# Second half's values as Strassen pairs behind ten split gate pairs, in a decoder block on one core

## The chip, the cores and the metric

The kernel runs on one core of a Trainium2 chip. The metric is the device time of one execution in microseconds; the figure for a kernel is the median of its runs. A profile is one further execution recorded by the hardware profiler; its span reaches from the first to the last instruction.

## The reference

One decoder block over 2048 positions and 1024 channels, in float32. `h` is the normalised and modulated input; one projection with eight column groups of 1024 feeds everything that follows:

```python
mod = c_act @ w_mod[l] + b_mod[l]
h = rms_norm(x, g_norm[l]) * (1.0 + scale) + shift
proj = h @ w_in[l]
x_rnn, z_rnn, q, k, v, z_attn, g_r, g_a = jnp.split(proj, IN_SPLITS, axis=-1)
...  # convolution and gated recurrence over x_rnn, times silu(z_rnn), projected
...  # rotary embedding of 32 of 128 channels of q and k, attention of 8 heads, times silu(z_attn), projected
merged = sigmoid(g_r + bg_r) * y_rnn + sigmoid(g_a + bg_a) * y_attn
x = rms_norm(x + gate * (merged @ w_o[l]), g_final)
```

## The kernel before

**Number format.** Every float32 operand is held as a high and a low part, and a product is three matmuls on TensorE (`mm3`, L156): high times high, high times low, low times high. The high part is a rounding copy on ScalarE (`hi_act`, L162); the low part is a subtraction, on GpSimd (`lo_pool`, L168) or on VectorE (`lo_dve`, L171).

**Halves and banks.** The positions are worked on in two halves (`for f in range(2)`, L1463), each of two banks of 512 positions, the even and the odd one. B11 and B21 hold the upper and lower 512 channels of the even bank of h, B12 and B22 those of the odd bank. Each is a high and a low tile of 128 x (4 x 512), from a pool of 14 such slots (`T`).

**Strassen pairs.** A projection's columns are taken 256 at a time, as a pair of 128-column blocks. With the two halves of the 1024 input channels and the two banks this is a 2 x 2 block product, made from seven block products instead of eight (`strassen`, L375). In order they use B11, T2, T3, T1, B21, T4 and B22; T1 to T4 are sums of the four B operands. The left operands (numbers 0 to 6 of the pair) are the blocks a11, a12, a21, a22 of w_in and their sums. A block product is 4 x 3 matmuls of 128 x 128 by 512 columns. Product 0 leaves a sum in PSUM bank X; ScalarE copies it to `u1` (L410), and product 4 goes on adding in X, four products later. u2 and u3 are Z + u1 and W + u2, on VectorE. Product 6 is held back until the next pair's product 0 is through (`behind`, `last_product`). `done(i, j, ps, u)` ends output block i for bank j.

**Order of the work.** Every engine's instructions stand in the order of the program (a manual schedule). `n_prod` counts block products; after each, `run_late` (L222) issues what was put down for that count in `late`, `after_prod` and `events`. `later(d, fn)` and `steps_after` put work down d products ahead.

**Left operands.** In the first half a pair's blocks are loaded from w_in, summed on VectorE and split into `S` tiles, a ring of seven (`s_tile`, L195), four products ahead (`LEAD`). Raw blocks go through a ring of five (`raw_tile`). The split operands are stored to `sD`, but for operands 0, 4 and 5, which are plain blocks of w_in and are loaded and split anew in the second half (`is_raw`, L270), and but for the two pairs of `ANEW`, whose operands are all made again. In the second half `load_next` (L326) loads operand n as soon as operand n - 7 is used, on the queue of SyncE (SP), and `split_next` splits raw ones four products ahead.

**The pairs.** 28 pairs a half: eight recurrent ones, twelve gate ones (silu gate and the two merge gates), six plain ones and two rotated ones of q and k; the same order in both halves. A recurrent pair sets off some 19 products of steps, among them two small products with `w_a` and `w_x` into the two `pg` banks of PSUM (L1033) and their sigmoids one product later (L1038).

**Values.** The 1024 value columns aren't pairs. `value_runs` (L904) makes them with positions as rows: a run is 256 columns for one bank, 96 matmuls with 256 moving columns. In the second half `second_values` (L927) does eight runs before the first pair: four on the even bank, then four on the odd one. Meanwhile `build_odd` (L567) turns the odd bank's x (`turned`, four transposes on TensorE), makes B12, B22 and T1 to T4 and splits them. Its low parts are on VectorE but for B12's and B22's share and T3, which is on GpSimd (L586). The even bank is built during the last pair of the first half (`next_even`, L1434). Under the value runs go also `residual_gate` (L1326), 16 pieces of w_mod summed on VectorE, and the loads of the value columns. `rotary_tables` (L1086) and `output_weights` (L451), which splits both output projections into `wD`, run under the second half's pairs.

Of the kernel before, what the change touches and what calls it, by code (L numbers as in the profile page):

```python
# [20 lines left out]
P = 128  # L21
# [5 lines left out]
H = 8  # L27
# [62 lines left out]
def decoder_block(ctx, tc, x, c, positions, g_norm, w_mod, b_mod, w_in, b_gate, conv_w, conv_b,  # L90
# [176 lines left out]
    ANEW = (22, 27)  # L267
    loaders, unsplit = {}, []

    def is_raw(x, i):  # L270
        return i in PLAIN and x in loaders and not (i == 5 and x + 1 in ANEW)


    def operand_events(x, pieces, f=0):
# [9 lines left out]
        def split(i, name):  # L284
            if f:
                assert n_loaded[0] == 7 * x + i
                n_loaded[0] += 1
# [38 lines left out]
    def load_next():  # L326
        n = n_loaded[0]
        n_loaded[0] += 1
        if n < 28 * 7:
            t = s_tile([P, 2, KH, P])  # L330
            if is_raw(n // 7, n % 7):
                unsplit.append((n, t, loaders[n // 7](*PLAIN[n % 7])))
            else:
                nc.sync.dma_start(t[:].bitcast(F32), sD[n])
            loaded.append((n, t))
        else:
            k = n - 28 * 7
            if k < 3:
                load_wd(0, 0, k) if k < 2 else load_wd(0, 1, 0)
# [9 lines left out]
    def load_free():  # L349
        n = n_loaded  # L350
        while n[0] - NS in used and not (n[0] < 28 * 7 and n[0] // 7 in ANEW):
# [23 lines left out]
    def strassen(up, f, key, done):  # L375

        x = pair_id[key]
        if f and x == 0:
            while n_loaded[0] < NS:
                load_next()  # L380
            split_next(4)
        n_op = iter(range(7 * x, 7 * x + 7))

        def take():
            if f and x not in ANEW:
                return (f, *loaded.pop(0))
            i = next(n_op)
            return f, i, first.pop(i)

        def prod(ps, b, first, last, op=None):  # L390
            f, i, s = op or take()
            bh, bl = B[b]
            for k in range(KH):
                mm3(ps[:], s[:, 0, k, :], s[:, 1, k, :], bh[:, k, :], bl[:, k, :],
                    first=first and k == 0, last=last and k == KH - 1, skip_group_check=True)
            n_prod[0] += 1
            if f:
                used.add(i)
                load_free()
                split_next(i + 4)  # L400
            run_late(n_prod[0])
            if f:
                load_free()
                split_next(i + 4)

        X = T(pj, [P, CH], F32, "X", bufs=2)
        prod(X, "B11", True, False)
        last_product()
        u1 = T(up, [P, CH], F32, "u1", bufs=1)
        nc.scalar.activation(u1[:], X[:], AF.Copy)  # L410
        Z = T(pj, [P, CH], F32, "Z")
        prod(Z, "T2", True, True)
        u2 = T(up, [P, CH], F32, "u2", bufs=2)
        with tc.high_priority():
            nc.vector.tensor_tensor(u2[:], Z[:], u1[:], ALU.add)
        W = T(pj, [P, CH], F32, "W")
        prod(W, "T3", True, True)
# [3 lines left out]
        V = T(pj, [P, CH], F32, "V")  # L421
        prod(V, "T1", True, False)
        done(1, 1, V, u3)
        prod(X, "B21", False, True)
        done(0, 0, X, None)
        Y = T(pj, [P, CH], F32, "Y")
        prod(Y, "T4", True, True)
        done(1, 0, Y, u3)
        op = take()

        def last():
            prod(V, "B22", False, True, op)
# [4 lines left out]
    behind = []  # L437

# [12 lines left out]
    def output_weights():  # L451

        parts = [(i, w, m, half) for i, w in enumerate((w_out_rnn, w_out_attn)) for m in range(KT) for half in range(2)]
        for x, (i, w, m, half) in enumerate(parts):
# [17 lines left out]
            for d, fn in ((1, load), (4, split), (6, store)):  # L472
                after_prod.setdefault(n_prod[0] + 9 * x // 2 + d, []).append(fn)
# [92 lines left out]

    def build_odd(st, xs):  # L567

        B["B12"] = (T(st, [P, KH, CH], F32R, "b12h"), T(st, [P, KH, CH], F32R, "b12l"))
        operand("B22")  # L570
        f32 = lambda b, i, k: B[b][i][:, k, :].bitcast(F32)
        tt = nc.vector.tensor_tensor
# [7 lines left out]

        low = []

        def split(name, k, t):
            hh, hl = (b[:, k, :] for b in B[name])
            hi_act(hh, t)
# [1803 lines left out]
```

## Time and profile before

| what | value |
|---|---|
| runs | 2186.95, 2187.05, 2190.51 us; median 2187.05 |
| profiled execution | span 2189.4 us; no separate time of it beside the span is given |
| TensorE busy | 2156.2 us (98%), 11333 matmuls |
| VectorE, ScalarE, GpSimd busy | 1494.8, 1266.5, 1237.3 us |
| DMA | 513.91 MB, mean 235 GB/s |
| second half's values | 697.7 to 795.6 us |
| second half's pairs | 795.6 to 1353 us |

In a row of the profile PE is TensorE's matmul, PEld its weight load, DVE VectorE, ACT ScalarE, POOL GpSimd and SP SyncE, whose queue issues most DMAs. L154 is a line of the kernel; a helper's line (L154, L162, L168, L171) stands for all its callers, so the tiles' names say which work it is. A group's row ends with busy time, mean duration in ns and the idle time before it. In the order of time, the first number is the start and the second the duration, both in us; matmuls are pipelined, so the pace of a group is the distance between starts.

### The profile page before, as it was taken

The numbers are of one execution on the slowest core, as the hardware profiler recorded it, in microseconds if no ns is written. First come the engines' busy times: TensorE is split into PE (matmuls) and PEld (weight loads), VectorE is DVE, ScalarE is ACT, GpSimd is POOL, SyncE is SP. The second block draws the span as 40 slices with busy tenths as digits, with TensorE's granted clock in tenths as the row PEclk, the third lists the DMA queues.
The fourth block names the chain that finished last, engine by engine and source line by source line (L and its number), as shares of the span: only waits on it lengthen the run. The fifth ranks groups of instructions, "written<-read, shape, count | busy, mean of one in ns | idle before, by whom it ended". The sixth has DMA issues, their size and how long they took to land.

```text
span 2189.4 us, 34270 instructions
## 1 busy us (share of the span) xinstructions
PE 2156.2 (98%) x11333; PEld 1834.3 (84%) x11333; DVE 1494.8 (68%) x2456; ACT 1266.5 (58%) x2544; POOL 1237.3 (57%) x909
## 2 busy tenths in 40 slices
PE   8999999999999999999999999999999999999998
PEld 6998888888888998888888888888989898978787
DVE  6779888978576765455536556567677778746877
ACT  4547667667543447557567412677778887632443
POOL 2467767677567355445444324456565656433886
PEclk9999999999999999999999999999999999999999
DMA  8355665665997567887887899989988788799554
GB/s 297 103 171 195 216 198 190 205 216 192 266 269 226 164 190 252 249 252 236 261 258 243 264 295 294 286 268 276 279 274 270 239 261 256 223 295 274 182 170 135
DMA packets 454474, 513.91 MB, mean 235 GB/s; under 512 B 91192, under 2 KB 333588, under 8 KB 453528
## 3 DMA queue, kind: packets, MB, share of 16 engines
q1 hardware_dynamic: 422644, 429.45, 65.4%
q10 hardware_dynamic: 31460, 82.22, 9.9%
q8 instruction: 90, 1.47, 0.3%
q14 instruction: 88, 0.72, 0.1%
q0 software_dynamic: 192, 0.05, 0.0%
HBM read 337.52 MB, written 174.07 MB: 234 GB/s over the span
## 4 chain that ended last, share of the span: by engine, by line
PE 62%; DMA 8%; DVE 5%; issue 2%; ACT 2%; POOL 1%; SPq 1%; DVEq 0%; ACTq 0%; POOLq 0%
PE X L154 12%; PE V L154 11%; PE pj L154 9%; PE W L154 6%; PE Z L154 6%; PE Y L154 6%; PE sc L154 4%; PE o L154 4%; PE pg L154 1%; DMA vraw<-vN 1%; PE pT L1708 1%; PE pT L1721 1%; DMA mrT<-fg 1%; DMA or<-in_w_o_dram 1%; DMA or<-oD 1%
## 5 line engine op out<-in xcount | busy, mean ns | idle before, releaser
L168 POOL TENSOR_TENSOR S<-R,S 128x512 fp32r<-128x512 f32 x278 | 413.0, 1491 | 378.2 <-ACT S L162 320.2
L154 PE MATMUL V<-T,S 128*128 128x512 f32 x1344 | 324.4, 390 | 0.6 <-DVE xr L481 0.6
L154 PE MATMUL X<-T,S 128*128 128x512 f32 x1344 | 323.3, 389 | 0.2 <-POOL S L168 0.2
L154 PEld LDWEIGHTS X<-T,S 128*128 128x128 f32 x1344 | 252.0, 188 | 52.8 <-POOL S L168 0.7
L154 PEld LDWEIGHTS V<-T,S 128*128 128x128 f32 x1344 | 251.4, 188 | 52.9 <-DVE xr L481 1.0
L154 PE MATMUL pj<-yh,S 128*128 128x512 f32 x848 | 284.1, 394 | 1.4 <-ACT yh L162 0.8
L162 ACT ACTIVATE S<-R 128x512 fp32r<-128x512 f32 x278 | 171.6, 624 | 134.9 <-DMA R<-in_w_in_dram 88.2
L168 POOL TENSOR_TENSOR S<-s,S 128x512 fp32r<-128x512 f32 x114 | 183.1, 1606 | 99.2 <-ACT S L162 70.1
L154 PEld LDWEIGHTS pj<-yh,S 128*128 128x128 f32 x848 | 159.2, 188 | 34.0 <-ACT yh L162 1.6
L1624 ACT ACTIVATE pp<-pp,st 128x256 f32<-128x256 f32 (+3 forms) x256 | 133.9, 526 | 74.1 <-DVE st L1623 73.7
L154 PE MATMUL pj<-yl,S 128*128 128x512 f32 x424 | 165.3, 392 | 1.3 <-POOL yl L168 0.9
L154 PE MATMUL Y<-T,S 128*128 128x512 f32 x672 | 161.5, 389 | 0.0
L154 PE MATMUL W<-T,S 128*128 128x512 f32 x672 | 161.5, 389 | 0.0
L154 PE MATMUL Z<-T,S 128*128 128x512 f32 x672 | 161.4, 389 | 0.0
L154 PEld LDWEIGHTS Z<-T,S 128*128 128x128 f32 x672 | 126.1, 188 | 26.2
L154 PEld LDWEIGHTS Y<-T,S 128*128 128x128 f32 x672 | 126.1, 188 | 26.1
L154 PEld LDWEIGHTS W<-T,S 128*128 128x128 f32 x672 | 126.1, 188 | 26.1
L162 ACT ACTIVATE S<-s 128x512 fp32r<-128x512 f32 x114 | 71.4, 626 | 125.7 <-DVE s L299 63.5
L171 DVE TENSOR_TENSOR ptl<-pT,pth 128x384 fp32r<-128x384 f32 (+1 forms) x160 | 97.8, 628 | 50.8 <-ACT pth L162 48.6
L1025 DVE SCALAR_TENSOR_TENSOR xc<-xr,par,xc 128x512 f32<-128x512 f32 x96 | 98.1, 1022 | 50.2 <-ACT xc L1019 47.9
L1623 DVE CUSTOM_DVE_ANT_0 pp<-sc,msk 128x256 f32<-128x256 f32 (+3 forms) x256 | 104.2, 449 | 33.0 <-PE sc L154 30.7
L1688 ACT ACTIVATE pp<-pp,M 128x256 f32<-128x256 f32 (+3 forms) x256 | 118.6, 528 | 9.2 <-DVE M L1812 9.2
(400 smaller groups left out, 4818.3 us busy)
## 6 DMA issues: line engine op xcount, KB each, us to landing
sD<-S ACTq DMA_DIRECT2D x112, 512.0 KB, 3.6
S<-sD SPq DMA_DIRECT2D x112, 512.0 KB, 5.0
S<-wD SPq DMA_DIRECT2D x100, 512.0 KB, 6.2
R<-in_w_in_dram SPq DMA_DIRECT2D x195, 256.0 KB, 4.3
wD<-s ACTq DMA_DIRECT2D x64, 256.0 KB, 4.4
T<-in_w_mod_dram SPq DMA_DIRECT2D x8, 1024.0 KB, 9.6
vN<-ev SPq DMA_DIRECT2D x64, 128.0 KB, 2.7
zaT<-ev SPq DMA_DIRECT2D x32, 256.0 KB, 3.6
```

Source lines behind the costliest of these rows:

```text
L154: nc.tensor.matmul(o, lhsT=l, rhs=r, start=st, stop=sp, **kw)
L162: nc.scalar.activation(o, i, AF.Copy)
L168: nc.gpsimd.tensor_tensor(o, i, h.bitcast(F32), ALU.subtract)
L171: nc.vector.tensor_tensor(o, i, h.bitcast(F32), ALU.subtract)
L1025: nc.vector.scalar_tensor_tensor(xc, xr[:, i : i + CH], cw(i), xc, ALU.mult, ALU.add)
L1623: nc.vector.tensor_tensor_reduce(pdst, s_ps, mask, 1.0, 3e38, ALU.add, ALU.min, m_)
L1624: nc.scalar.activation(pdst, pdst, AF.Exp, bias=m_, scale=-1.0, accum_out=l_)
L1688: nc.scalar.activation(pp, pp, AF.Copy, scale=w)
L1708: nc.tensor.transpose(pt[:, c0 + j * P : c0 + (j + 1) * P], pp[i][:, k * P : (k + 1) * P], ident)
L1721: nc.tensor.transpose(pt[:, c * P : (c + 1) * P], pp[:, half * P : (half + 1) * P], ident)
```

## The change

In the second half the values become four pairs (`("v", m)`) of seven products each. An output block of such a pair has channels as rows; it is evicted, turned by four transposes into a `pg` bank two products later, copied by ScalarE and stored (`value_done`). Their left operands are made anew from w_in (`ANEW`).

The second half starts with `second_heads`: ten of the twelve gate pairs do only their products 0 and 4, those with B11 and B21, two pairs at a time (X, X or Z, W). The first sums are kept in ten `u1h` tiles. These 20 products take the place of the value runs as the time in which the odd bank is built. `build_odd_late` makes no B12, takes 16 steps (after head products 6 to 21) and a rest after product 22, splits what a step made one and two products later, and gives the low parts of T1, T2 and T3 to GpSimd. Then the ten pairs' remaining five products follow (`strassen` with `u1`), with a changed use of PSUM banks (`body_tags`). `residual_gate`, `output_weights` (every 4 products instead of 4.5) and `rotary_tables` run under these. The remaining order of the second half is new: each recurrent pair is followed by one other, the last by two.

The loads of x for the odd bank and of the first seven operands move into the last pair of the first half. `ops2` lists the second half's operands in their order of use; `sD` is indexed by pair and operand.

```diff
-    ANEW = (22, 27)
+    N1 = 28 * 7
+    ANEW = (22, 27, 28, 29, 30, 31)
...
+    def heads(up, f, pairs):
+        U = []
+        Xs = [T(pj, [P, CH], F32, tag, bufs=1 + (tag == "X")) for tag in next(head_tags)]
+        for X, (key, _) in zip(Xs, pairs):
+            prod(take(f, pair_id[key], 0), X, "B11", True, False)
+            U.append(T(up, [P, CH], F32, "u1h", bufs=N_HEADS))
+            nc.scalar.activation(U[-1][:], X[:], AF.Copy)
+        for X, (key, done) in zip(Xs, pairs):
+            prod(take(f, pair_id[key], 4), X, "B21", False, True)
+            done(0, 0, X, None)
+        return U
+
+    def strassen(up, f, key, done, u1=None):
+        x, X = pair_id[key], None
+        if u1 is None:
+            X = T(pj, [P, CH], F32, "X", bufs=2)
+            prod(take(f, x, 0), X, "B11", True, False)
+            last_product()
+            u1 = T(up, [P, CH], F32, "u1", bufs=1)
+            nc.scalar.activation(u1[:], X[:], AF.Copy)
...
+        last_product()
...
+        tag = "V" if X is not None else next(body_tags)
+        V = T(pj, [P, CH], F32, tag, bufs=1 + (tag == "X"))
...
+    N_HEADS = 10
+    ODD_AT = tuple(range(6, 22))
+    body_tags = itertools.cycle(("V", "X", "X"))
+    head_tags = itertools.cycle((("X", "X"), ("Z", "W")))
...
-                after_prod.setdefault(n_prod[0] + 9 * x // 2 + d, []).append(fn)
+                after_prod.setdefault(n_prod[0] + 4 * x + d, []).append(fn)
...
+    def build_odd_late(st, up, xs):
...
+        def step():
+            ready = then[:]
+            then.clear()
+            for fn in soon:
+                then.append(fn())
+            soon.clear()
+            for fn in ready:
+                fn and fn()
+
+        def halves(name, k, t, low=True):
+            def hi():
+                hi_act(B[name][0][:, k, :], t)
+                return (lambda: lo_pool(B[name][1][:, k, :], t, B[name][0][:, k, :])) if low else None
+            soon.append(hi)
+
+        for k in range(KH):
+            build(st, ("B12", "B22"), xs, KH + k, keep=h[k])
+            pt = turned(xs, k)
+            nc.scalar.activation(h1s[:, k, :], pt[:].rearrange("p r j -> p (r j)"), AF.Identity,
+                                 bias=sh[:, k : k + 1], scale=gs[:, k : k + 1])
+            yield
...
+        for part, k in ("a0", "b0", "a1", "b1", "a2", "b2", "a3", "b3", "c0", "c1", "c2", "c3"):
...
+            if part == "a":
+                t = T(st, [P, CH], F32, "t0", bufs=2)[:]
+                tt(t, h2, h1, ALU.subtract)
+                tt(h1, h1, stored("B11", 0, k), ALU.subtract)
+                tt(h1, h1, stored("B11", 1, k), ALU.subtract)
+                step()
+                halves("T3", k, t)
+                halves("T1", k, h1)
+            elif part == "b":
+                tt(h2, h2, h1, ALU.subtract)
+                step()
+                halves("T2", k, h2)
+            else:
+                tt(h2, stored("B21", 0, k), h2, ALU.subtract)
+                tt(h2, h2, stored("B21", 1, k), ALU.add)
+                step()
+                halves("T4", k, h2, False)
+            yield
+        step()
+        B["T4"] += (slot(),)
+        for k in range(KH):
+            (lo_dve if k % 2 else lo_pool)(B["T4"][1][:, k, :], h[k], B["T4"][0][:, k, :])
...
+        plan[4].append(lambda: rstd_last(ss))
+        for r in range(4):
+            plan[2 + r // 2].append(lambda r=r: square(r))
+            plan[4 + r // 2].append(lambda r=r: scale_rows(x3, ss, range(r, r + 1)))
...
+    def value_done(up, f, m):
+        def value(i, j, ps, u):
+            n, v = 2 * f + j, {}
+            t0 = plain_at[0]()
+            wait = scaled(t0, ps, u, 1.0)
+            def turn():
+                v["pt"] = T(pg, [P, 4, P], F32, "pg")
+                for r in range(4):
+                    nc.tensor.transpose(v["pt"][:, r, :], t0[:, r * P : (r + 1) * P], ident)
+            def store():
+                t = plain_at[0]()
+                nc.scalar.activation(t[:], v["pt"][:].rearrange("p r d -> p (r d)"), AF.Copy)
+                nc.sync.dma_start(vN[2 * m + i, :, n * P : (n + 1) * P, :].rearrange("r j d -> j r d"),
+                                  t[:].rearrange("p (r d) -> p r d", r=4))
+            steps_after(n_prod[0], ((wait + 1, turn), (wait + 2, store)))
+        return value
...
+    others2 = [1, 1, 1, 1, 1, 1, 1, 2]
+    TAIL2 = [rotated_keys[0], value_keys[3], rotated_keys[1], rest[0], rest[-1]]
+    for i in range(0, N_HEADS, 2):
+        ops2 += [(pair_id[key], op) for op in (0, 4) for key in head_keys[i : i + 2]]
+    ops2 += [(pair_id[key], op) for key in head_keys[:N_HEADS] for op in (1, 2, 3, 5, 6)]
+    ops2 += [(pair_id[key], op) for key in (*ORDER2, *TAIL2) for op in range(7)]
...
         def at_slot(i, fn):
-            plan[i // 4, i % 4].append(fn)
+            later(i + 6, fn)
...
-        for i in range(4):
-            later(3, lambda i=i: load_piece(0, i))
-            later(4 + i, lambda i=i: (split_piece(0, i), load_piece(1, i)))
+        for i in range(2):
+            def load(i=i):
+                t = T(hp, [P, 2, D], F32, "T", bufs=14)
+                nc.sync.dma_start(t[:], xv[3, 2 * i : 2 * i + 2].rearrange("r j d -> j r d"))
+                x3.extend((t[:, 0, :], t[:, 1, :]))
+            later(4 + i, load)
+        for i in range(NS):
+            late.setdefault(N1 + 1 + i - NS, []).append(load_next)
+            late.setdefault(N1 + 2 + i - NS, []).append(lambda i=i: split_next(i))
...
         if f:
             pools.close("xp")
...
-            vx = pools.open("vx", bufs=1)
-            second_values()
+            hu = pools.open("hu", bufs=1)
+            st = pools.open("st", bufs=1)
+            U = second_heads(hu, st)
+            output_weights()
+            residual_gate(hu)
+            rotary_tables(hu, f)
+            for key, u1 in U.items():
+                strassen(hu, f, key, gate_done(hu, f, *key), u1)
+            last_product()
+            finish_late()
+            pools.close("st", "hu")
```

391 lines of the change are left out of this document (200 added, 191 removed).

## The prediction

> **What bounds the kernel now.** I read the head of the page first, then busy times by stage over the second half's projections, then the order of time on TensorE in the stage that goes.
>
> ```profile
> span 2189.4 us, 34270 instructions
> PE 2156.2 (98%) x11333; PEld 1834.3 (84%) x11333; DVE 1494.8 (68%) x2456; ACT 1266.5 (58%) x2544; POOL 1237.3 (57%) x909
> ...
> PE 62%; DMA 8%; DVE 5%; issue 2%; ACT 2%; POOL 1%; SPq 1%; DVEq 0%; ACTq 0%; POOLq 0%
> ```
>
> ```profile
> core 0: us, PE busy (x) PEld busy (x) DVE busy (x) ACT busy (x) POOL busy (x), PEclk, DMA share, GB/s
> 697.60:748.60 51.00, 50.84 (x421) 49.76 (x420) 29.79 (x39) 24.54 (x42) 17.58 (x13) 1.00 0.65 207
> 748.60:795.60 47.00, 47.00 (x389) 46.00 (x389) 43.80 (x42) 20.09 (x36) 26.36 (x17) 1.00 0.43 128
> 795.60:1000.00 204.40, 204.16 (x902) 168.72 (x901) 101.97 (x129) 124.29 (x200) 99.14 (x74) 1.00 0.81 252
> 1000.00:1200.00 200.00, 200.00 (x892) 165.59 (x891) 103.67 (x136) 130.41 (x212) 99.43 (x73) 1.00 0.82 253
> 1200.00:1353.00 153.00, 153.00 (x677) 126.68 (x676) 87.99 (x115) 42.68 (x70) 51.61 (x35) 1.00 0.90 284
> ```
>
> TensorE works without a gap at a granted clock of 1.00, from the value sums (the first two rows) to the last pair. So a microsecond of its work taken out here shortens the kernel by one, and every wait put in lengthens it. Two covers are thin: VectorE is busy 43.80 of 47.00 us while it builds the T operands, and DMA runs at 0.81 to 0.90 of its time once pairs run.
>
> **The change, part by part.** TensorE in order of time, at the places that give prices:
>
> ```profile
> 680.87 0.60 PE L541 MATMUL pg<-cs,x 128*128 128x128 f32 x4
> ...
> 684.07 0.60 PE L541 MATMUL pg<-cs,x 128*128 128x128 f32 x4
> ...
> 697.67 1.68 PE L154 MATMUL X<-S,T 128*128 128x256 f32 x12
> 699.19 1.60 PE L154 MATMUL Z<-S,T 128*128 128x256 f32 x12
> 700.63 1.60 PE L154 MATMUL X<-S,T 128*128 128x256 f32 x12
> ...
> 731.49 1.02 PE L154 MATMUL pg<-s,ones 128*1 128x512 f32 x2 [0.16 <-DVE s L1347]
> ...
> 794.15 1.60 PE L154 MATMUL X<-S,T 128*128 128x256 f32 x12
> 795.60 0.63 PE L154 MATMUL X<-T,S 128*128 128x512 f32 x2
> 796.46 2.58 PE L154 MATMUL X<-T,S 128*128 128x512 f32 x10 [0.24 <-POOL S L168]
> 798.88 2.88 PE L154 MATMUL Z<-T,S 128*128 128x512 f32 x12
> 801.60 2.88 PE L154 MATMUL W<-T,S 128*128 128x512 f32 x12
> ```
>
> *Removed:* eight value runs of 96 matmuls, 256 columns wide: 64 groups of twelve. A group starts 700.63 - 699.19 = 1.44 us after the last, so 92.2 us; the stage's 97.9 us (697.67 to 795.60) hold besides the eight turns of the odd bank and four one-row matmuls, which stay. With the stage go its two idle spots, 0.16 and 0.24 us.
>
> *Added:* four pairs of seven products. A product of twelve 512-column matmuls takes 801.60 - 798.88 = 2.72 us, so 28 are 76.2 us. Each of the 16 outputs is turned by four transposes; such a turn and the product behind it take 684.07 - 680.87 = 3.20 us, so a turn costs 0.48 us and 16 cost 7.7. TensorE's work thus falls by 92.2 + 0.4 - 76.2 - 7.7 = 8.7 us. That is the whole gain; the rest is what the new order takes back.
>
> The odd bank was built under 97.9 us of value sums; now it must be built under 20 head products, 54.4 us, before the first T product. Prices for that:
>
> ```profile
> L168 POOL TENSOR_TENSOR S<-R,S 128x512 fp32r<-128x512 f32 x13 | 20.8, 1614 | 33.0 <-ACT S L162 32.9
> L168 POOL TENSOR_TENSOR T<-t,T 128x512 fp32r<-128x512 f32 x4 | 6.5, 1630 | 1.3 <-ACT T L162 1.3
> ...
> L162 ACT ACTIVATE S<-R 128x512 fp32r<-128x512 f32 x13 | 7.8, 623 | 0.3 <-issue 0.3
> ```
>
> ```profile
> 785.99 1.75 POOL L168 TENSOR_TENSOR T<-t,T 128x512 fp32r<-128x512 f32 x1
> ...
> 795.12 1.29 POOL L168 TENSOR_TENSOR S<-R,S 128x512 fp32r<-128x512 f32 x1 [3.99 <-ACT S L162]
> ```
>
> ```profile
> 763.00 0.69 DVE L593 TENSOR_TENSOR hx<-hx,T 128x512 f32<-128x512 f32 x1
> 763.61 0.68 DVE L171 TENSOR_TENSOR T<-t,T 128x512 fp32r<-128x512 f32 x1
> ...
> 786.61 1.67 DVE L600 TENSOR_TENSOR hx<-hx,hx 128x512 f32<-128x512 f32 x1
> 788.32 1.66 DVE L603 TENSOR_TENSOR t<-T,hx 128x512 f32<-128x512 f32 x1
> ```
>
> A subtraction of two SBUF tiles takes 1.29 us on GpSimd alone and 1.75 beside VectorE; on VectorE 0.69 alone (0.61 from start to start) and 1.67 beside GpSimd.
>
> *T operands late.* Count from the end of head product 10. The steps run after products 10 to 21, and a piece's low part follows two products after its subtractions. After product 12 (at 5.4 us) GpSimd gets, in order, five splits of head operands (the lead is four products, so they end after product 16) and the twelve low parts of T3, T1, T2, which `build_odd` gave mostly to VectorE. The first waits for ScalarE's 0.62, so they start at 6.0; 17 at the mean of 1.63 end at 33.7. T2's last low part is read by the eleventh of product 21's twelve matmuls, at 27.2 + 2.27 = 29.5: 4.2 us late. At 1.29 it is in time (27.9, nothing); at 1.75 it is 6.3 late. VectorE has 16 subtractions after product 12, a partner for nearly every GpSimd one, so I take 4.2. T4 is late next, and needs nothing more: its last subtraction is emitted after product 21, three products ahead.
>
> [...]
>
> *Start of the heads.* Seven operands are fetched in the last seven products of the first half, one `S` tile each; the first lands in the ring ahead of the last pair's operands 5 and 6. So the sixth takes the first one's slot, which is free only after head product 1. ScalarE waits there, at 2.7 us, and queued behind it are the split (0.62), two high parts of B21, another split, and the copy of the first X, without which product 3 (at 5.4 us) may not write.
>
> ```profile
> 697.52 1.45 ACT L551 ACTIVATE T<-pg,mod,gs 128x512 fp32r<-128x512 f32 x2 [2.42 <-PE pg L541]
> ...
> 821.03 0.58 ACT L410 ACTIVATE u<-X 128x512 f32<-128x512 f32 x1
> ```
>
> 2.7 + 2 x 0.62 + 1.45 + 0.58 = 6.0: 0.6 us late. Below, nothing, should the split come sooner; above some 4, since two 1 MB loads of x now lie on SP's queue ahead of those operands, and such loads take 9.0 us to land. The scaling of x's rows, which `second_values` did in its second run, has four products here and I give it nothing.
>
> *DMA under the ten bodies.*
>
> ```profile
> S<-sD SPq DMA_DIRECT2D x112, 512.0 KB, 5.0
> R<-in_w_in_dram SPq DMA_DIRECT2D x195, 256.0 KB, 4.3
> wD<-s ACTq DMA_DIRECT2D x64, 256.0 KB, 4.4
> ...
> grT<-ev SPq DMA_DIRECT2D x32, 256.0 KB, 4.1
> ...
> T<-in_x_dram SPq DMA_DIRECT2D x4, 1024.0 KB, 9.0
> gw<-in_w_mod_dram SPq DMA_DIRECT2D x16, 256.0 KB, 3.8
> ```
>
> A body of five products loads four operands of 512 KB and one of 256, and stores three tiles of 256; the output weights add a 256 KB load and two 256 KB stores every four products. That is 826 kB a product, 304 GB/s; and for 16 products the residual gate, moved here from the value stage, adds 262 kB: 400 GB/s. The stage rows give 252 / 0.81 = 311, 309 and 316 GB/s at full share. Those 16 products need 17.4 MB, of which 2.8 MB (six operands) are fetched ahead: 14.6 MB at 310 take 47.1 us against 43.5. Cost: 0 if the weights alone run late, 3.6 if the operands do; both stand in one queue, so 1.8.
>
> *Value pairs.* A value output's turn falls, behind recurrent blocks 6 and 7, on the product after which both `pg` banks are filled by gate sums; the transposes wait for a sigmoid.
>
> ```profile
> 823.36 0.39 PE L154 MATMUL pg<-xh,gh 128*128 128x512 f32 x1
> ...
> 824.72 2.88 PE L154 MATMUL V<-T,S 128*128 128x512 f32 x12
> ```
>
> ```profile
> L1038 ACT ACTIVATE y<-pg,par 128x512 f32<-128x512 f32 x15 | 10.3, 688 | 7.6 <-PE pg L154 7.6
> ```
>
> The six gate matmuls take 1.36 us, the first bank is full at half of it, and its sigmoid takes 0.69: at best no wait, with one ScalarE operation ahead 0.6. Twice, 0 to 1.5; I take 0.8.
>
> Costed at nothing: the rotary tables and the gate's sums on VectorE (busy 101.97 of 204.40 us where they go; without that cover 16 sums at 0.69 to 1.67 are 11 to 27 us), output weights every 4 instead of 4.5 products, recurrent blocks every 14 products (GpSimd 99, ScalarE 124 of 204 us), B12 no longer made.
>
> Sum: -8.7 + 4.2 + 0.6 + 1.8 + 0.8 = -1.3 us. It is made against a span of 2189.4 us; the runs took 2186.95 to 2190.51, so this execution is an ordinary one, and what lies around a span has no row. Off the median of 2187.05: **2185.8 us**.
>
> **Rivals.** *The build fits* (faster): GpSimd keeps near 1.29 us because VectorE's share is small (24 subtractions in 33 us; `build_odd` had 36 in 45), and DMA delays only weights. Then 2187.05 - 8.7 + 0.6 + 0.8 + 1 = 2180.8. Against it: the 1.63 mean was measured beside more VectorE work but at 26.36 of 47.00 us GpSimd busy; here it would be full.
>
> [...]
>
> *DMA sets the pace of the bodies* (slower): all 50 body products need 50 x 0.826 + 4.2 - 2.8 = 42.7 MB within 136 + 4.2 us. Above 305 GB/s they fit; below it TensorE starves, and SP's queue, waiting for a gate piece, holds operands back. The stage rows sit at 309 to 316, just above; at 285, midway to the 253 actually moved, it takes 149.8 us: 9.6 - 1.8 more than mine, 2193.6. Against it: no idle time in the 204.16 of 204.40 us at 0.81.
>
> **How the numbers follow.** A measurement of this kernel can tell about 0.2%, 4.4 us, from no change. Chances: forecast 0.37, build fits 0.33, exclusion 0.09, DMA 0.21. So faster 0.33, same 0.46, slower 0.21. Low end: the 8.7 us with every joint near its lower bound, 2179; high end past the DMA case with T late by 6.3 instead, 2195. The forecast's own range is 2183 to 2191.
>
> **What would show it.** The value stage gone and 28 more products at 2.72 us; turns at about 0.5 us; TensorE busy less by about 8 us. T late: idle in the first body's Z, ended by GpSimd's T2 low parts, and GpSimd full from head product 12 on. Start: a short idle before the third head product, ended by ScalarE. DMA: share near 1 under the bodies, and TensorE's idle there ended by `sD` loads. I am wrong if the heads run without a gap (then faster), or if idle time in the bodies exceeds 6 us (slower).

## The result, and the profile after

The changed kernel is 0.6% slower: 2201.39 us median (four runs, 2198.38 to 2203.79) against 2188.11 us (four runs) beside it, a ratio of 1.0060 with a 95% interval of 1.0045 to 1.0074. The prediction, 2185.8 us in a range of 2179 to 2195, missed it by 15.6 us. Run again as the base of the experiments ("the repeat" below) it came out at 2202.92 us and 1.0062 (1.0048 to 1.0077).

The profiled execution took 2198.38 us. The head of its page:

```profile
span 2196.6 us, 33538 instructions
PE 2151.2 (98%) x10964; PEld 1811.2 (82%) x10965; DVE 1532.0 (70%) x2478; ACT 1262.5 (57%) x2547; POOL 1257.4 (57%) x919
```

TensorE has 5.0 us less work and the span is 7.2 us longer. The busy time by stretch, first of the changed kernel (heads, bodies, blocks, tail), then of the kernel before at the end of the pairs:

```profile
core 0: us, PE busy (x) PEld busy (x) DVE busy (x) ACT busy (x) POOL busy (x), PEclk, DMA share, GB/s
697.60:752.00 54.40, 52.20 (x245) 42.43 (x246) 37.52 (x39) 35.95 (x62) 33.36 (x23) 1.00 0.48 137
752.00:900.00 148.00, 143.11 (x623) 115.49 (x623) 76.11 (x111) 41.94 (x66) 47.46 (x34) 0.99 0.91 303
900.00:1200.00 300.00, 300.00 (x1331) 248.40 (x1330) 174.11 (x200) 196.16 (x321) 158.41 (x116) 1.00 0.78 238
1200.00:1320.00 120.00, 117.59 (x541) 96.38 (x541) 83.75 (x97) 56.14 (x93) 55.87 (x38) 1.00 0.63 196
1320.00:1352.00 32.00, 32.00 (x143) 26.50 (x142) 31.74 (x35) 8.37 (x15) 22.79 (x13) 1.00 0.75 200
```

```profile
1320.00:1352.00 32.00, 32.00 (x143) 26.50 (x142) 23.25 (x28) 6.79 (x12) 15.10 (x10) 1.00 0.96 311
```

Nothing is lost from 900 to 1200 us. It is lost where stages meet: under the heads, in the first bodies, in the tail. The view of TensorE's waits over this stage names them (after, then before):

```profile
engine line waited for: us in total, times, longest us
PE pj L155 <- ACT yh L163: 3.3, 1, 3.3
PE Z L155 <- POOL T L169: 2.1, 1, 2.1
PE pg L155 <- DVE ga L1471: 1.7, 1, 1.7
PE V L155 <- DVE t L501: 1.5, 1, 1.5
PE X L155 <- ACT u1h L409: 1.5, 2, 1.1
PE pg L561 <- DVE t L581: 1.2, 2, 0.7
PE pg L1343 <- ACT ev L1347: 0.7, 1, 0.7
PE pg L561 <- DVE T L881: 0.6, 1, 0.6
PE X L155 <- POOL T L169: 0.3, 1, 0.3
```

```profile
PE X L154 <- POOL S L168: 0.2, 1, 0.2
PE pg L154 <- DVE s L1347: 0.2, 1, 0.2
```

12.9 us of waits stand where 0.4 stood. And a wait can cost more than its length. TensorE in order of time, at three of these places, and the first product behind the pairs in the kernel before:

```profile
765.94 0.73 PE L155 MATMUL Z<-T,S 128*128 128x512 f32 x2 [2.13 <-POOL T L169]
766.51 4.50 PE L155 MATMUL W<-T,S 128*128 128x512 f32 x12
...
810.78 1.02 PE L155 MATMUL pg<-ga,ones 128*1 128x512 f32 x2 [1.67 <-DVE ga L1471]
811.73 3.06 PE L155 MATMUL W<-T,S 128*128 128x512 f32 x12
...
1359.20 0.61 PE L155 MATMUL pj<-yh,S 128*128 128x512 f32 x2
1363.07 5.16 PE L155 MATMUL pj<-yh,S 128*128 128x512 f32 x14 [3.26 <-ACT yh L163]
```

```profile
1352.97 3.90 PE L154 MATMUL pj<-yh,S 128*128 128x512 f32 x16
```

The product behind the wait of 2.13 us takes 4.50 instead of 2.88 us: eight of its matmuls start 0.427 us apart instead of 0.227, which is half rate (the granted clock reads 0.50 there, in the last section), and lose 1.6 us. Behind 3.26 us the same happens: fourteen matmuls take 5.16 us, and at the pace of the twelve behind the wait of 1.67 us (3.06 us, no half rate) they would take 3.5, so another 1.6 us are lost. The pairs end at 1359.20 instead of 1352.97, 6.2 us later. Lined up by VectorE's instructions, the changed kernel is 11.4 us behind after the wait for yh, 9.3 us where attention has begun (1423 us), and gets 2 us back by the end.

The wait for yh was in no term of the sum. ScalarE at that place (ACTq is its queue), after and before:

```profile
1352.19 0.33 ACTq L1525 DMA_DIRECT2D oD<-ws  x1
1355.62 0.34 ACTq L1526 DMA_DIRECT2D oD<-wo  x1
...
1362.38 3.75 ACT L163 ACTIVATE yh<-T 128x512 fp32r<-128x512 f32 x7 [5.13 <-DMA oD<-wo]
```

```profile
1344.24 0.33 ACTq L1402 DMA_DIRECT2D oD<-wo  x1
...
1352.33 2.20 ACT L162 ACTIVATE yh<-T 128x512 fp32r<-128x512 f32 x4 [3.48 <-DMA oD<-wo]
```

yh takes over memory that the gated weight's last store still reads. In the kernel before that store is issued 8.7 us ahead of the pairs' end, in the changed one 3.6 us. Two things could have done this: the store's place in the order (product 33 of a tail of 35, before 39 of 42), or VectorE, which makes what is stored and is busy 31.74 of 32.00 us there instead of 23.25.

### The profile page after: what moved, and what is told of

Same layout as the page of the kernel before. It is cut to its first block, busy times and chain, and to the rows that moved or that the text cites. A ratio compares the mean times of both kernels' runs of the same rounds, so it can differ in the third digit from the quotient of the medians.

```text
span 2196.6 us, 33538 instructions
## 1 busy us (share of the span) xinstructions
PE 2151.2 (98%) x10964; PEld 1811.2 (82%) x10965; DVE 1532.0 (70%) x2478; ACT 1262.5 (57%) x2547; POOL 1257.4 (57%) x919
## 5 line engine op out<-in xcount | busy, mean ns | idle before, releaser
L169 POOL TENSOR_TENSOR S<-R,S 128x512 fp32r<-128x512 f32 x266 | 395.5, 1492 | 321.2 <-ACT S L163 280.7
L155 PE MATMUL X<-T,S 128*128 128x512 f32 x1488 | 358.4, 390 | 1.8 <-ACT u1h L409 1.5
L155 PEld LDWEIGHTS X<-T,S 128*128 128x128 f32 x1488 | 278.2, 188 | 61.6 <-ACT u1h L409 2.7
L155 PE MATMUL V<-T,S 128*128 128x512 f32 x1296 | 313.3, 391 | 2.5 <-DVE t L501 1.5
L169 POOL TENSOR_TENSOR S<-s,S 128x512 fp32r<-128x512 f32 x126 | 201.1, 1596 | 114.1 <-ACT S L163 85.6
L155 PE MATMUL Z<-T,S 128*128 128x512 f32 x768 | 185.4, 390 | 2.1 <-POOL T L169 2.1
L155 PE MATMUL W<-T,S 128*128 128x512 f32 x768 | 186.6, 392 | 0.0
L155 PE MATMUL Y<-T,S 128*128 128x512 f32 x720 | 173.2, 389 | 0.0
L155 PEld LDWEIGHTS W<-T,S 128*128 128x128 f32 x768 | 145.0, 189 | 31.1 <-issue 0.9
L155 PEld LDWEIGHTS Z<-T,S 128*128 128x128 f32 x768 | 143.7, 188 | 32.2 <-POOL T L169 2.6
```

The source lines that it names most:

```text
L155: nc.tensor.matmul(o, lhsT=l, rhs=r, start=st, stop=sp, **kw)
L169: nc.gpsimd.tensor_tensor(o, i, h.bitcast(F32), ALU.subtract)
```

## The experiments

The theory: each wait stands on the path, and mending one returns its length and the half rate behind it. The rivals: waits only pass to the next joint, or memory sets the pace. Ratios are against the kernel before, run beside each. A difference of two ratios is uncertain by about 0.002, or 4 us.

| run | edit of the changed kernel | us | ratio, 95% interval |
|---|---|---|---|
| a0_after | none (the repeat) | 2202.92 | 1.0062, 1.0048 to 1.0077 |
| a3_start | loads around the start | 2199.51 | 1.0038, 1.0026 to 1.0051 |
| c1_t1_behind_t2 | start; T1 queued behind T2 | 2200.15 | 1.0039, 1.0025 to 1.0054 |
| c4_without_tail | the same; first gate total later | 2198.49 | 1.0040, 1.0028 to 1.0052 |
| a4_sum_turn | gate totals and a turn later | 2206.09 | 1.0075, 1.0059 to 1.0091 |
| e2_no_pieces | 14 gate pieces not loaded | 2197.56 | 1.0036, 1.0023 to 1.0050 |
| b2_store | last store two products earlier | 2202.35 | 1.0061, 1.0049 to 1.0074 |
| b4_early_start_store | start, store, build a product earlier | 2199.56 | 1.0043, 1.0031 to 1.0056 |
| a2_tail6 | tail of 42, value pair first | 2208.74 | 1.0083, 1.0069 to 1.0097 |
| c2_tail42 | start; tail of 42, rotated pair first | 2206.62 | 1.0073, 1.0062 to 1.0085 |
| c3_all_three | c4's and c2's edits | 2206.66 | 1.0075, 1.0062 to 1.0088 |
| d3_sums_gpsimd | c4's; store earlier, sums on GpSimd | 2205.56 | 1.0072, 1.0057 to 1.0086 |
| d4_both_totals | d3's; second gate total later | 2208.35 | 1.0085, 1.0070 to 1.0100 |
| e1_no_gate | gate not multiplied in | 2198.89 | 1.0043, 1.0031 to 1.0055 |
| b1_heads12 | twelve split pairs | 2236.37 | 1.0208, 1.0190 to 1.0226 |
| b3_heads12_start_store | twelve, start, store | 2227.98 | 1.0173, 1.0159 to 1.0187 |
| d1_before_store1 | kernel before, store a product later | 2188.10 | 0.9988, 0.9979 to 0.9997 |
| d2_before_store2 | kernel before, two products later | 2191.83 | 1.0009, 1.0000 to 1.0019 |

**The repeat.**

> The changed kernel again, on the same chip as its variants. Theory (joints): 8.7 us of TensorE's work is gone, and about 18 us of waits and half-rate stretches stand at the places where stages meet; so 2198 to 2204 us again, 1.0045 to 1.0075 of the kernel before, and an execution's time goes up as its granted clock goes down (.996 at 2198, .993 at 2204). Rival (another chip or moment): within 0.2% of the kernel before.

As expected. Six executions show granted clocks of .991 to .995, those of the kernel before .994 to .999.

**The start of the heads.**

```
-  later(4 + i, load)                       # x's two 1 MB loads
+  later(3, load)
-  for i in range(NS): load_next at N1 - 6 + i, split_next(i) one product later
+  load_next at N1 - 4, -4, -3, -2, -1, 0, 0; split_next(0..2) at N1 - 2, -1, 0
```

> x's two 1 MB loads are issued one and two products earlier, the seven first operands are loaded behind the last splits of the first half so that the first no longer takes a ring slot ahead of that half's last operands, and only three of them are split early. Theory (joints): the short waits of turns 6 and 7 (excess 1.6 us), of head products 3 and 4 (1.1 us) go, and some of the 0.7 us behind x's rows: 2.5 to 3.3 us under the changed kernel. Rival (T's low parts on GpSimd set the first body's start whatever the heads do): what the heads gain is waited for at T2, 0 to 0.7 us. Rival (clock): 0.

3.4 us under the repeat (5.3 by the ratios, with some 4 of uncertainty): the theory held, and the rival's 0 to 0.7 lies just outside. What went is seen in ScalarE's order of time. Changed kernel:

```profile
691.68 0.63 ACT L163 ACTIVATE S<-R 128x512 fp32r<-128x512 f32 x1 [4.48 <-DMA R<-in_w_in_dram]
...
695.08 0.63 ACT L163 ACTIVATE S<-R 128x512 fp32r<-128x512 f32 x1 [2.10 <-DMA R<-in_w_in_dram]
...
702.65 0.63 ACT L163 ACTIVATE S<-R 128x512 fp32r<-128x512 f32 x1 [4.60 <-PE X L155]
```

The third row is the ring conflict that the prediction described. The first two were left in its upper bound: blocks of w_in land late, x's loads standing ahead of and between them on SP's queue, and the even bank's last turns, queued behind these splits, wait. With the edit ScalarE still waits 4.22 us for a block, but TensorE has no wait left before 745 us. The 1.1 us at a later head's X, which waits for ScalarE's copy `u1h`, stay.

**T2's low parts.** Three edits went at the wait of 2.1 us. The first two gave more time to the build:

```
-N_HEADS = 10
+N_HEADS = 12            # heads 11 and 12 leave the recurrent part; output weights every 3.5 products;
                         # the silu gate's sigmoids use the "gw" tiles; the heads start in banks Z, W
```

> Twelve gate pairs are split instead of ten, so the odd bank is built under 24 head products instead of 20; the last two gate pairs no longer stand among the recurrent blocks, and the output weights come every 3.5 products. Theory (T's low parts on GpSimd are 2.1 us late after 20 products): four more products of 2.72 us cover it; the wait of 2.13 us for T2 and the 1.4 to 1.6 us at half rate behind it go, and the wait of 1.09 us for the copy of a head with them or not: 3.5 to 5 us under the changed kernel (2198 to 2199.5). Rival (the build's pace hangs on the head products, whose splits share GpSimd, so it grows with them): half of it, 0 to 2 us. Rival (the denser recurrent part pays): it waits there instead, and the time stands within 1 us or rises, as it did with the pair moved into the tail.

> Twelve split gate pairs, the earlier x loads and regrouped first operands, and the gated weight's last store two products earlier, together. Theory (joints, each independent): -3.4 measured for the start, -4.5 for the store, -3.5 to -5 for the heads: 11.4 to 12.9 us under the changed kernel, about 2190 to 2191.5, even with the kernel before (ratio 0.9995 to 1.001). Rival (waits only move to the next joint): half of it at most, 2196 or more.

Both miss by far. T2's wait fell to 0.4 us, but others came in. The largest waits in the first of the two:

```profile
PE pg L155 <- ACT xh L163: 8.7, 1, 8.7
PE V L155 <- DVE t L501: 8.2, 1, 8.2
PE X L155 <- ACT u1h L409: 7.9, 1, 7.9
```

The last comes from my sharing of tiles: a sigmoid waited for the build to leave a `gw` tile and stood ahead of ScalarE's copy of a head. The first stands behind the last recurrent pair, which no other pair follows now: two sets of its small gate products come one right behind the other, and the second waits for ScalarE's high part. The second is the tail's VectorE. So these runs don't price the heads.

The third edit only changes GpSimd's order (on top of the start's):

```
+ if name == "T1" and k > 1: t1_low.append(fn)      # issued behind T2's last low part
```

> On top of the earlier x loads and regrouped first operands (-3.4 us against the changed kernel), the low parts of T1's last two pieces are queued on GpSimd behind T2's last one instead of ahead of it. No work is added or removed. Theory (GpSimd works at 1.70 us an operation in its own order and is the bound; T2 is read first, T1 two products later): T2's last low part ends 3.4 us sooner, so the wait of 2.13 us and the 1.56 us at half rate behind it go, at the risk of some 0.2 us for T4: 3.5 to 3.9 us under the run with the start alone (2199.5), so 2195.6 to 2196, and TensorE shows no half rate in the first body. Rival (VectorE's subtractions pace it, so the order on GpSimd is nothing): 0. Rival (what is won at a joint is waited for at the next, as with the store alone): 0 to 1.5.

The wait for T2 and the half rate behind it are gone: GpSimd's order was the cause. But the time stayed (1.0039 against 1.0038). T4's low parts, on VectorE, are late instead, and in the profiled execution the gate's sum too:

```profile
PE pg L155 <- DVE ga L1478: 3.5, 1, 3.5
...
PE Y L155 <- DVE T L172: 1.7, 1, 1.7
```

The rival (the wait passes on) holds here: both engines are full in this stretch (from 738 to 766 us of the changed kernel VectorE is busy 27.62 and GpSimd 28.00 of 28.00 us), so the last operand of the four is late whichever comes first.

> Ten split pairs, with the start and the store as in the run beside it, and x's squares, scaling and all sixteen steps of the odd bank one head product earlier. Theory: T2's low parts end 2.7 us earlier while their reader stays, so the wait of 2.13 us goes and the half rate behind it too; with start (-3.4) and store (-4.5) that is 11 to 12 us under the changed kernel, 2191 to 2192. Rival (x's rows land or are scaled too late for a step earlier): a wait of up to 2.7 us at the first turn of the odd bank takes its place, 2193 to 2195. Rival (GpSimd's queue starts from a fixed point): T2 stays late, 2195.

```
-ODD_AT = tuple(range(6, 22))
+ODD_AT = tuple(range(5, 21))       # squares and scaling a product earlier too; start's edit, store's edit
```

Nothing gained on the start alone (1.0043 against 1.0038). T2 still waits 1.5 us, and x's rows 0.7: GpSimd and VectorE pace the build, not the head products.

**The gate's sum.**

```
-at_slot(10 + 9 * q, total), (12 + 9 * q, bias)
+at_slot(13 + 9 * q, total), (15 + 9 * q, bias)     # a4; and the turn of output (0,1) a product later
+at_slot(12 + 7 * q, total), (14 + 7 * q, bias)     # c4: the first half only
```

> The residual gate's total and bias come three products later, and the turn of a value output (0,1) one product later. Theory (joints): the waits of 1.67 us for the gate sums and of 1.4 us in all at the value turns go: 2.5 to 3.3 us under the changed kernel. Rival (DMA sets the pace of the bodies): the late gate pieces were a symptom, operands come late in their place, and no more than 1.4 us is gained. Rival (clock): 0.

> The same without the tail's edit: start, T1 behind T2, and the first total of the residual gate two products later. Theory: the end of the pairs keeps its wait of 3.2 us and the half rate behind it, so the time lies 4 to 6 us above the run with the tail's edit, at 2193.5 to 2195; against the run without the gate's edit it gains 1 to 1.7 us. Rival (the tail is not worth its wait): within 1 us of the run with it.

In a4 the first sum's wait is gone, but 1.2 us appear at an X that waits for VectorE, 1.0 at a turn of the tables and, from nothing in the edit that I can name, 2.8 instead of 1.2 us at the start; the time did not fall. In c4 the wait went from the first total to the second, 1.6 us. It gained nothing that can be told from the run without it. So the place of the totals was not the lever; the pieces' landing was tried next:

```
+ if k: w[q, k] = w[q, 0]; return        # one piece of each half loaded, used eight times
```

> The changed kernel with one of eight pieces of the residual gate's weight loaded for each half, and used eight times: 14 loads of 256 KB less under the bodies, the additions stay. So this kernel leaves out seven eighths of the gate's weight. Theory (the gate's first sum waits because its pieces land late, 1.67 to 2.5 us, and nothing else there waits for transfers): 1.7 to 2.5 us under the changed kernel, 2200.4 to 2201.2. Rival (transfers under the bodies pace more than that one wait): 4 us or more less. Rival (the wait passes on): 0.

5.4 us under the repeat, 5.7 by the ratios, with some 4 of uncertainty. The wait of 1.7 us is gone and nothing else changed in that stretch of the profile, where DMA moved 284 GB/s at a share of 0.88 instead of 303 at 0.91. The expected 1.7 to 2.5 lies within the interval, and so does the rival's 4.

**The end of the pairs: place or load?**

```
-for k, i in enumerate((1, 9, 17, 25)):
+for k, i in enumerate((1, 9, 16, 23)):
```

> Of the changed kernel only the gated weight's groups are moved: they start after products 1, 9, 16 and 23 of the tail instead of 1, 9, 17 and 25, so the last store is issued 5.4 us earlier. Theory (yh reuses the memory that this store still reads): the wait of 3.2 to 3.3 us at the first product behind the pairs and the 1.2 to 1.7 us at half rate behind it go: 4 to 5 us under the changed kernel (about 2198 to 2199). Rival (memory is full there, share .93): another load is late in its place, 0 to 1 us. The run with 42 products in the tail speaks for the theory: neither wait nor half rate stood there, though the kernel lost more elsewhere.

Nothing gained. yh's wait of 3.3 us went, but VectorE's waits in the tail grew from 1.5 to 2.8 us, and loads right behind the pairs were waited for. The place alone was then tried on the kernel before:

```
-for k, i in enumerate((1, 11, 21, 31)):      # kernel before
+for k, i in enumerate((1, 11, 21, 32)):      # and with 33
```

> The kernel before with one number changed: the last of the gated weight's four groups starts after product 32 of its 42-product tail instead of 31, so its store is issued two products ahead of the end, as in the changed kernel, instead of three. Theory (yh waits for this store's transfer, and there is no slack: in the kernel before ScalarE already waited 3.48 us for it): TensorE waits up to 2.7 us at the end of the pairs, with or without 1.2 to 1.6 us at half rate behind it: 1.5 to 4.5 us over the kernel before. Rival (the joint is full of memory traffic whatever the store does): within 1 us of the kernel before.

> The same with 33: the store is issued one product ahead of the end. Theory: the wait is 5.4 us and the half rate behind it is sure: 5.5 to 7.5 us over the kernel before, so the joint's price grows by a product for a product. Rival (memory): within 1.5 us.

My theory fell: a product later cost nothing (0.9988), two products later at most 0.2% (1.0009). With 32 the store was issued at 1345.85, with 33 at 1348.14 us, both still early enough, because in a manual schedule a product's number sets an order and not a time: with 31 and 32 ScalarE's queue runs ahead to the store, which is issued 0.03 us after VectorE's last subtraction ends (1344.21 and 1345.82); with 33 it stands behind ScalarE's copy of an X at 1347.66. So what VectorE has to do in the tail was to be changed:

```
 def gate(i):
-    tt(v[i], v[i], gate_b, ALU.mult)
+    pass
```

> The changed kernel without the eight multiplications of the output weight by the gate on VectorE (1.2 to 1.8 us each); the loads, the subtractions and the stores stay. So this kernel leaves out the gate's factor on the output weight. Theory (VectorE is full at the end of the tail, 31.74 of 32.00 us against 23.25 before, so the last subtractions end late, the store behind them is issued at 1355.6 instead of 1344.2 us, and yh waits for it): the wait for yh of 3.2 us, the half rate behind it and VectorE's 1.5 to 1.9 us at the head of the tail go: 4 to 6 us under the changed kernel, 2197 to 2199. Rival (the tail's length or memory sets that joint, whatever VectorE does): 0 to 1 us.

4.0 us under the repeat (4.2 by the ratios). VectorE's busy time in the last 32 us falls, the wait in the tail is gone, and yh waits 1.4 us with no half rate behind:

```profile
1320.00:1352.00 32.00, 32.00 (x143) 26.50 (x142) 26.84 (x32) 8.26 (x15) 20.18 (x13) 1.00 0.81 224
```

Against the rival speaks also that DMA's share there had fallen from 0.96 to 0.75 in the changed kernel. The intervals (1.0048 to 1.0077, 1.0031 to 1.0055) still touch, so the amount is uncertain, not the place. And VectorE isn't all that holds the store. In the changed kernel its last subtraction ends at 1353.97, but the store is issued at 1355.62, when a store of q, issued at 1346.06, has landed (1355.53):

```profile
ACT t L1260 <- DMA qT<-t: 7.8, 1, 7.8
```

Without the multiplications these times are 1350.26, 1352.88 and 1352.79. So the last 1.6 us (2.5 in e1) before the store are a transfer's. No run moved that store of q alone.

**A longer tail, or GpSimd.** Four layouts were to give VectorE more room:

```
-others2 = [1, 1, 1, 1, 1, 1, 1, 2];  TAIL2 = [rotated0, v3, rotated1, rest0, rest3]
+others2 = [1, 1, 1, 1, 1, 1, 1, 1];  TAIL2 = [v2, rotated0, v3, ...]            # a2
+                                     TAIL2 = [rotated0, v2, rotated1, v3, ...]  # c2, c3
+ the gated weight at (1, 11, 21, 31) in both
```

> One value pair moves out of the recurrent part into the tail, so the tail has 42 products again instead of 35, and the gated weight starts its four groups after products 1, 11, 21 and 31, its last store three products ahead of the end instead of two, at the old spacing of ten products. Theory (joints): TensorE's wait of 3.26 us for yh at the end of the pairs, the 1.20 us it then loses at half rate and the wait of 1.52 us for VectorE in the tail go, and nothing takes their place: 4.5 to 6 us under the changed kernel. Rival (memory sets the pace of that stage, DMA share .93 there): the yh tile comes no earlier or another transfer is late in its place, 0 to 1 us. Rival (the clock is lower throughout, for a reason that no wait gives): 0 to 1 us.

> On top of the start's edit, the third value pair moves from the recurrent part to the tail, behind the first rotated pair, and the gated weight's groups start after products 1, 11, 21 and 31 as in the kernel before. The earlier run that put this pair first in the tail had no wait at the end of the pairs (-1.1 us from there to 1423 us against +3.1 to +8.2 in the changed kernel), but lost 5.6 + 1.8 us where the next pair's operands queued behind the tail's other loads, and 2.4 us at a turn. Theory: with the rotated pair first, as in the changed kernel, its operands are fetched in time, and the end's gain stays: 4 to 6 us under the run with the start alone (2199.5), so 2193.5 to 2195.5. Rival (the recurrent part or the tail's loads pay for it again): 2199 or more.

> Start, T1 behind T2, the 42-product tail, and the first total and bias of the residual gate two products later. Theory (the changed kernel's loss is the sum of these joints, and each can be mended alone): -3.4, -3.7, -5 and -1.7 against the changed kernel, 2188 to 2190, not slower than the kernel before. Rival (some joints only pass their wait on): 2192 to 2195. Rival (granted clock: the new order itself costs half-rate stretches wherever it stands): 2193 or more with a mean clock still at .993 to .995 against .996 before.

In all three the wait for yh went, and in all three the tail's opening cost more. In a2 the next pair's operands stood on SP's queue behind the gated weight's loads; in c2 VectorE's multiplication by the gate, which waited 4.44 us for its load, stood ahead of the rotated pair's sums:

```profile
1269.31 5.15 PE L155 MATMUL X<-T,S 128*128 128x512 f32 x12 [5.43 <-DMA S<-sD]
```

```profile
PE V L155 <- DVE t L501: 5.3, 1, 5.3
PE pg L1343 <- ACT t L1347: 2.5, 1, 2.5
PE pg L155 <- ACT ev L1347: 2.4, 2, 1.7
```

```
-tt(...)                          # the sixteen subtractions of the gated weight
+nc.gpsimd.tensor_tensor(...)     # with the start, T1, first total and store edits
```

> The changed kernel with the start, T1 behind T2 and the first total later (2198.5 us), and now the gated weight's last store two products earlier with its sixteen subtractions on GpSimd instead of VectorE, so that VectorE's work between the stores does not grow denser. Theory (the store is the cause at the end of the pairs; moving it alone only passed the wait to VectorE's 1.5 us and to the loads behind): the waits for yh (3.7 us) and for VectorE in the tail (1.3 us) and a stretch at half rate (1.6 us) go: 4 to 6 us less, 2192.5 to 2194.5. Rival (the loads behind the pairs wait for memory in its place, as where the store was moved alone, 1.4 + 1.2 + 1.6 us): 0 to 2 us less.

> The same with the second total and bias of the residual gate two products later as well. Theory (the 1.8 us passed from the first total to the second, because the pieces land late): another 1 to 1.8 us less than the run beside it. Rival (VectorE or the tables' turns take it over, as with three products): 0.

The load only changed its engine: in d3 VectorE fell to 21.65 of 32.00 us, GpSimd rose to 27.54, and operand splits, which are GpSimd's, now came late as well; yh's waits sum to 5.0 us:

```profile
1320.00:1352.00 32.00, 30.33 (x126) 24.29 (x125) 21.65 (x25) 8.14 (x15) 27.54 (x19) 0.95 0.68 196
```

In d4, with both totals later, no total is waited for, but 2.9 us of X waiting for VectorE come in, and the time is no lower than in d3 (1.0085 against 1.0072). Neither version beats the kernel before, nor does any other of the changed order.

## Why the prediction was wrong

**TensorE's work (-8.7): right.** Busy time fell by 5.0 us, but half rate is in it. Counted by the median distance of starts of each shape (0.227 us for 512 columns), the matmuls from the even bank's last turns (691 us) to the pairs' end take 653.0 us instead of 661.9: 8.9 less.

**T operands late (+4.2): right in mechanism, near in size in part by luck.** GpSimd's seventeen operations were as counted, at 1.67 instead of 1.63 us each (first and last of them):

```profile
737.44 1.29 POOL L169 TENSOR_TENSOR S<-R,S 128x512 fp32r<-128x512 f32 x1 [1.81 <-ACT S L163]
...
764.17 1.71 POOL L169 TENSOR_TENSOR T<-gw,T 128x512 fp32r<-128x512 f32 x1
```

TensorE waited 2.1 us, half of what was forecast, in part because the heads were themselves late (1.1 us at an X that waits for `u1h`, in no term); it lost 1.6 more at half rate, which no term held either. "T4 is late next, and needs nothing more" was wrong: with T2 mended it cost 1.7 us. What the chances call exclusion (0.09) is shown by no run; from the first one's start to the last one's end the seventeen took 28.4 us.

**Start of the heads (+0.6): mis-sized.** It measured 3.4 us by a3. The conflict in the ring was there as told; the late blocks of w_in behind x's loads stood only in the bound.

**DMA under the bodies (+1.8): nearly the size, by another way.** No operand came late. The residual gate's pieces did, and its first sum, a matmul in TensorE's order, waited 1.7 us for them; the prediction had looked at "the weights alone" and operands, not at who waits for a piece. The DMA rival priced starvation of operands, which did not happen, so its 2193.6, the nearest of the forecasts to the measured time, was so for a reason that wasn't there.

**Value turns (+0.8):** 0.7 us in the waits, and 0.3 us twice by the starts.

**What failed: the part "costed at nothing".** The gated weight, 42 products of tail made 35, was not in it at all. Its work and the rotated pairs' lie on VectorE, and the cover quoted for the tables and sums, 101.97 of 204.40 us, is the mean of another stretch. In the tail the cover was gone: VectorE full, 1.5 us of wait at its head and 3.3 + 1.6 at the end. Taking the multiplications out returned 4.0 us (4.2 by the ratios, with some 4 of uncertainty).

**What also failed: a wait taken at its length.** The sum counts idle time. By the granted clock of all executions on one chip, .9961 before (eleven) and .9935 after (six), and their mean spans of 2188 and 2202 us, (1 - clock) x span is 8.5 and 14.3 us: up to 5.8 of the 13.8 us between them are time at half rate (an upper bound, since idle time at a low clock is in it). The profiled execution, at .996 the fastest of its four, shows only 7.2 us.

**The sum, redone.** Up to the pairs' end the view of waits and the half rate give 9.6 + 1.6 = 11.2 us. From start to start the matmuls lose more, in part because the overlap of two matmuls is lost at each wait (one takes 0.39 us, the next starts 0.227 us after it): 12.6 us at the waits, 1.6 at half rate, 0.9 around turns and 0.3 elsewhere, 15.3 in all before rounding, against 0.2 in the kernel before. 15.1 - 8.9 = 6.2 us, the delay of the pairs' end. The wait for yh and its half rate come behind it.

**Not settled.** That later stages give back 2 us wasn't tried. Why e2's gain came out above its wait isn't shown, and where in an execution without a profile the clock is low can't be seen.

## What to carry to other kernels

When a change makes a stage shorter, look at what each other engine must still do in it, in a window at that stage's end, and not in the mean over the whole: here VectorE went from 23 to 32 of 32 us, because the gated weight's work came closer together (four of its multiplications in the window instead of two). When TensorE is full, count for each joint not only the wait but the half rate that may follow it (here behind 25 of 38 waits of 2.0 to 2.4 us). And when two engines are full together, reordering one of them may only change which operand is late, as here (1.0039 against 1.0038).

## What the runs showed of the hardware

How long must TensorE stand still until it goes on at half rate? The granted clock (PEclk) answers it when it is read in windows of 3.41 us. First the wait of 2.13 us in the changed kernel, then the same wait at the same place, 2.11 us, in the run with the store moved (b2):

```profile
763.35:766.77 3.42, 1.29 (x7) 0.73 (x6) 3.39 (x3) 1.18 (x3) 3.42 (x3) 1.00 0.26 102
766.77:770.18 3.41, 3.41 (x10) 2.63 (x9) 3.38 (x3) 0.66 (x2) 3.41 (x3) 0.50 0.44 154
```

```profile
763.04:766.46 3.42, 1.66 (x8) 1.04 (x6) 3.39 (x3) 1.12 (x2) 3.42 (x3) 1.00 0.45 153
766.46:769.87 3.41, 3.06 (x13) 2.55 (x14) 3.38 (x3) 0.63 (x1) 3.41 (x3) 1.00 0.32 101
```

```profile
766.81 0.73 PE L155 MATMUL Z<-T,S 128*128 128x512 f32 x2 [2.11 <-POOL T L169]
767.38 2.89 PE L155 MATMUL W<-T,S 128*128 128x512 f32 x12
```

The first wait lies in one window, and TensorE is busy 1.29 of its 3.42 us; the next window runs at half rate. The second is split between two windows, busy 1.66 and 3.06 us, and the product behind it takes 2.89 us instead of 4.50. In time the windows lie on a fixed grid: in each of the twenty profiles, between 600 and 2150 us, half rate begins only at points that lie whole numbers of 3.413 us apart (in the changed kernel at 766.77 and 1364.10, 175 of them, and for one such window each time). All windows at full clock in this stretch, over the twenty profiles:

| TensorE's busy share of the window | windows | half rate in the next |
|---|---|---|
| under 0.45 | 69 | 69 |
| 0.45 to 0.60 | 71 | 22 |
| 0.60 and more | 8825 | 1 |

So the length of a wait alone doesn't decide it. Half rate was granted within 3.41 us behind 4 of 20 waits of 1.6 to 2.0 us, 25 of 38 of 2.0 to 2.4 us and 32 of 33 of 3.0 us and more. A window at half rate can cost half its length, 1.7 us, by an estimate from its 3.413 us and a granted clock of 0.50; behind the waits of 2.13 and 3.26 us it cost 1.6 us each. What decides between 0.45 and 0.60 isn't shown.
